# Up projection in runs of sixteen products of one width, and three buffers moved

## Chip, cores and metric

The kernel runs on one core of a Trainium2 chip. The metric is the device time of one execution in microseconds. A core has a matrix engine (TensorE, PE in the profile; its weight loads are PEld), a vector engine (DVE), a scalar engine (ACT), GpSimd (POOL) and a queue engine (SP) that here only issues DMAs. Each engine works through its own list of instructions in order and waits on semaphores for the others.

## The reference

Two layers. Each has a mixer (attention and a short convolution, with their projections) and then the part that this change touches, a squared-ReLU MLP. The sequence is 256 tokens, the model width 2048, the hidden width 8192, all in float32:

```python
for l in range(DEPTH):                      # DEPTH = 2
    h = _rmsnorm(x, attn_norm_g[l])
    ...                                     # attention and short convolution of h @ w_in[l]
    x = x + jnp.concatenate([attn, conv.astype(attn.dtype)], axis=-1) @ w_out[l]

    hm = _rmsnorm(x, mlp_norm_g[l]) @ w_up[l]          # (256, 2048) @ (2048, 8192)
    x = x + jnp.square(jax.nn.relu(hm)) @ w_down[l]    # (256, 8192) @ (8192, 2048)
```

## The kernel before

**Precision by parts.** A float32 operand is split into a high part `hi` (a rounded copy, made on ACT) and a low part `lo` (the rest, a subtraction on DVE that needs `hi`). A product of two such operands is made of three matmuls: high by high, high by low, low by high. For the up projection this is folded: the activations' high and low parts stand side by side, so one matmul with 512 columns multiplies the weights' high part with both (the wide product), and one with 256 columns multiplies the weights' low part with the activations' high part (the narrow product). Both go into the same PSUM bank, `upc`.

**The up stage** (`mlp`, from L999). It runs over 32 pairs `i` of hidden blocks. A pair has two columns `c` of 128 hidden units. A column sums over 16 blocks of 128 input features, in two halves `kh` of eight. `up_part(acc, kh)` (L942) takes one weight tile pair (`uhi`, `ulo`, made by `column`, L807, from a raw tile `uraw`) and issues eight wide and then eight narrow products (L952). So a column is eight wide, eight narrow, eight wide, eight narrow. `evict` (L960) copies the bank to `ev` on ACT (L962), which frees it, and adds its halves into `h` on DVE (L963). There is one such bank, so `ev` must be done before the next column starts. The first pair (`i == 0`) has its four half columns in another order, each with a call of its own.

After both columns `square` (L965) works on `h`, the tile of unrounded units: ReLU, a scale, a square, four sums `S1` to `S4`, for some pairs (`SEVEN`) a store of `h` to memory on POOL's queue (L982), and the rounding into `f` (L984 on ACT, L985 on DVE). `h` has one buffer.

**The quarters.** Two pairs later (`LAG = 2`), the units `f` are multiplied with two 128-row blocks of `w_down` over the first 1024 of its 2048 columns, by a scheme of seven products instead of eight (`product`, L992; matmuls at L995, tiles `pr`): products 1, 2, 3, 5 behind the pair's first column and 7, 6, 4 behind its second, each of three matmuls. Their weights come from `quarters` (L834) in three steps: `plain` loads the raw tile `draw` (L829, two DMAs of 512 KB on SP) and makes the plain parts `b1` and `b2`; `sums` makes the sums `t` and from them `t13`; `more` makes `t24`. Parts are made at L842 (ACT) and L843 (DVE). The raw tile is free after the last sum (L860). Before the change there are two raw tiles, two buffers of `b1` and `b2` each, and one of `t`, `t13` and `t24` each.

**The down stage** (from L1083) does what is left of the down projection: ordinary products (L1077, L1152) and, for the pairs in `SEVEN`, quarters over the other 1024 columns, with `h` loaded back into a tile `back` of the same pool and tag as `h`.

**What sets the order.** `weights.take()` (L357) hands out weight tiles in a fixed order of jobs and also lets the jobs up to three ahead be written (`AHEAD = 3`). High and low tiles have three buffers each. PE's instructions stand in the order of the program (`manual_schedule`). Those of the other engines, DMA issues included, are put in order when the kernel is built, by a scheduler that simulates the timeline; `late` (and `keep`) pins single instructions in program order. `work.tick()` lets pieces of background work go on; beside the up stage there is little of it.

Of the kernel before, what the change touches and what calls it, by code (L numbers as in the profile page):

```python
# [9 lines left out]
F32 = mybir.dt.float32  # L10
# [5 lines left out]
P = 128  # L16
# [12 lines left out]
CH = 512  # L29
WC = 256  # L30
KG = 4
# [74 lines left out]
def trunk(ctx: ExitStack, tc: tile.TileContext, x, w_in, w_out, conv_w, q_norm_g, k_norm_g,  # L106
          lambda_q1, lambda_k1, lambda_q2, lambda_k2, subln_g, attn_norm_g, mlp_norm_g,
          w_up, w_down, rel_bias, selector, out):
    nc = tc.nc
# [16 lines left out]
    def bank(name):  # L126
        return ps.tile([P, CH], F32, tag="bank", name=name)
# [4 lines left out]
    work = Background()  # L132
# [657 lines left out]
    def mlp(l, mnorm, last):  # L790
# [4 lines left out]
        mT = mnorm.tiles  # L795
        with ExitStack() as scope:
            upool = scope.enter_context(tc.tile_pool(name="upool", bufs=4))
            fpool = scope.enter_context(tc.tile_pool(name="fpool", bufs=2))
            dpool = scope.enter_context(tc.tile_pool(name="dpool", bufs=2))
            spool = scope.enter_context(tc.tile_pool(name="spool", bufs=1))  # L800
            work.start(mnorm.factors(), 1)

# [1 line left out]
            weights = Weights(upool)  # L804
            raws, forms = {}, {}
# [20 lines left out]
            def load_rows(i, col, pool=dpool, tag="draw"):  # L826
                raw = pool.tile([P, 2, 2 * CH], F32, tag=tag, name=tag)
                for k in range(2):
                    nc.sync.dma_start(  # L829
                        raw[:, k], w_down[l][(i * 2 + k) * P:(i * 2 + k + 1) * P,  # L830
                                             col:col + 2 * CH])
                return raw

            def quarters(i, col=0):  # L834


                keep = late if i == 0 or (i == SEVEN[0] and col) else lambda ins: None

                def parts(src, tag, bufs):
                    hi = spool.tile(list(src.shape), F32R, tag=f"{tag}h", name=f"{tag}h", bufs=bufs)  # L840
                    lo = spool.tile(list(src.shape), F32R, tag=f"{tag}l", name=f"{tag}l", bufs=bufs)
                    keep(nc.scalar.activation(hi, src, AF.Copy))  # L842
                    keep(nc.vector.tensor_sub(lo, src, hi.bitcast(F32)))  # L843
                    return hi, lo

                def plain():
                    raw = forms["raw"] = load_rows(i, col).rearrange("p k (n c) -> p k n c", n=2)
                    h1, l1 = parts(raw[:, 0, 0], "b1", 2)
                    h2, l2 = parts(raw[:, 1], "b2", 2)
                    return (h1, l1), (h2[:, 0], l2[:, 0]), (h2[:, 1], l2[:, 1])  # L850

                def sums():
                    raw = forms["raw"]
                    t = forms["t"] = spool.tile([P, 4, CH], F32, tag="t", name="t")

                    keep(nc.vector.tensor_sub(t[:, 0:2], raw[:, :, 1], raw[:, 0]))  # L856
                    h, lw = parts(t[:, 0:2], "t13", 1)

                    keep(nc.vector.tensor_add(t[:, 2], t[:, 1], raw[:, 0, 0]))
                    keep(nc.vector.tensor_sub(t[:, 3], raw[:, 1, 0], t[:, 2]))  # L860
                    return (h[:, 0], lw[:, 0]), (h[:, 1], lw[:, 1])

                def more():
                    h, lw = parts(forms["t"][:, 2:4], "t24", 1)
                    return (h[:, 0], lw[:, 0]), (h[:, 1], lw[:, 1])

                if (i, col) == (0, 0):
                    made = {}
                    forms["plain"] = lambda: made.update(p=plain())
                    forms["sums"] = lambda: made.update(s=sums())  # L870
                    return lambda: made["p"], lambda: made["s"], more
                return plain, sums, more

            def rows(i, k, box, col=0, *where):
# [63 lines left out]
            def column_bank():  # L938
                acc = ps.tile([P, CH], F32, tag="av", name="upc", bufs=1)
                return acc.rearrange("p (h s) -> p h s", h=2)  # L940

            def up_part(acc, kh):  # L942

                hi, lo = weights.take()
                for part, wt in ((0, hi), (1, lo)):
                    for k in range(8):
                        a = mT[kh * 2 + k // KG]
                        while not a.ready:  # L950
                            work.tick()
                        nc.tensor.matmul(  # L952
                            acc[:, 0] if part else acc, wt[:, k],
                            a.ap[:, 0, k % KG] if part else a.ap[:, :, k % KG],
                            start=(part == 0 and kh == 0 and k == 0),
                            stop=(part == 1 and kh == 1 and k == 7), skip_group_check=True)
                        if k % 4 == 3:
                            work.tick()

            def evict(acc, dst):  # L960
                ev = nat.tile([P, 2, S], F32, tag="wide", name="ev")
                nc.scalar.activation(ev, acc, AF.Copy)  # L962
                nc.vector.tensor_add(dst.rearrange("p a c -> p (a c)"), ev[:, 0], ev[:, 1])  # L963
# [35 lines left out]
            for i in range(NP):  # L999
                j = i - LAG  # L1000
                end = i == NP - 1
                h = fpool.tile([P, 8, P], F32, tag="h", name="h", bufs=1)
                if i == 0:
                    two = mm.tile([P, 2, CH], F32, tag="mm2", name="up0")
                    two = [two[:, c].rearrange("p (h s) -> p h s", h=2) for c in range(2)]
                    for kh in range(2):
                        for c in range(2):
                            up_part(two[c], kh)
                    forms["plain"]()
                    for c in range(2):  # L1010
                        evict(two[c], h[:, 2 * c:2 * c + 2])
                    fs[0] = square(0, h)
                    forms["sums"]()
                    continue
                for c in range(2):
                    if i < LAG:
                        acc = bank("upw").rearrange("p (h s) -> p h s", h=2)
                    else:
                        acc = column_bank()
                    up_part(acc, 0)  # L1020
                    up_part(acc, 1)
                    evict(acc, h[:, 2 * c:2 * c + 2])
                    if c == 1:
                        fs[i] = square(i, h)
                    if j == 0 and c == 0:
                        for pair in ((1, 6), (2, 3)):
                            w2 = mm.tile([P, 2, CH], F32, tag="mm2", name=f"pr{l}{pair[0]}")
                            prods[pair[0]], prods[pair[1]] = w2[:, 0], w2[:, 1]
                        for n in (5, 7, 4):
                            prods[n] = bank(f"pr{l}{n}")  # L1030
                    if j >= 0 and c == 0:
                        b11, b21, b22 = weights.take()
                        t1, t3 = weights.take()
                        f = fs[j]
                        product(1, f, A11, b11, j == 0, end)
                        product(2, f, A12, b21, j == 0, False)
                        product(3, f, S4, b22, j == 0, False)
                        product(5, f, S1, t1, j == 0, end)
                        work.tick()
                    elif j >= 0:  # L1040
                        t2, t4 = weights.take()
                        f = fs[j]
                        product(7, f, S3, t3, j == 0, end)
                        product(6, f, S2, t2, j == 0, end)
                        product(4, f, A22, t4, j == 0, False)
                        work.tick()
# [45 lines left out]
            def pair(i, f=None, at=0):  # L1092

                if f is None:
                    f = apool.tile([P, 2, 8, P], F32R, tag="a", name="fb")
                if i not in SEVEN:
                    nc.gpsimd.dma_start(
                        f[:, :, at:at + 4].rearrange("p a k c -> p a (k c)"), hid[i])
                    return f
                back = fpool.tile([P, 8, P], F32, tag="h", name="back", bufs=1)  # L1100
                nc.gpsimd.dma_start(back.rearrange("p a c -> p (a c)"), hid7[i])
                nc.scalar.activation(f[:, 0], back, AF.Copy)
                nc.vector.tensor_sub(f[:, 1], back, f[:, 0].bitcast(F32))
                return f
# [56 lines left out]
            for i in range(2 * BLK):  # L1161
# [7 lines left out]
                start, end = i == SEVEN[0], i == SEVEN[-1]  # L1169
# [89 lines left out]
```

## Time and profile before

| | us |
|---|---|
| median of 3 runs | 2139.8 (2139.35 to 2141.16) |
| the profiled execution, its own time | 2141.08 |
| its span, first to last instruction | 2139.3 |
| PE busy | 2130.0 |
| DVE busy | 1700.6 |
| ACT busy | 1317.1 |
| mean granted clock of TensorE | 1.000 |

In the profile the up stage of the first layer lies from about 391 to 895 us, that of the second from about 1454 to 1957. Busy time of PE is modelled: matmuls overlap, so a busy PE may still have products that stand further apart than need be. A row of the order of time gives start, length, engine, line, operation, `out<-in`, shape and count; in square brackets stands the idle time of the engine just before it and what ended it. A row of the stretches gives, for each engine, busy time and count, then the granted clock, the share of the DMA engines and GB/s.

### The profile page before, as it was taken

The page shows a single profiled execution, that of the slowest core. Times are in us where ns is not written, and L with a number is a line of the kernel's source. Part 1 is how long each engine was busy: PE and PEld are TensorE (multiplying, and loading weights), DVE is VectorE, ACT ScalarE, POOL GpSimd, SP SyncE. Part 2 cuts the span into 40 slices and gives each one's busy share as a digit, 9 for nine tenths or more (in the row PEclk, how much of TensorE's full clock was granted, in tenths as well). Part 3 has the DMA queues.
Part 4 walks back from the last instruction along what each step waited for, and adds up shares of the span by engine and source line. Part 5 has one row for each costly group of instructions (what it writes and reads, how often), then busy time and mean ns, then how long its engine had stood idle before and what let it go on. Part 6 is the DMA issues. An engine that isn't in the chain of part 4 may idle for free.

```text
span 2139.3 us, 29295 instructions
## 1 busy us (share of the span) xinstructions
PE 2130.0 (100%) x10925; PEld 1817.7 (85%) x10925; DVE 1700.6 (79%) x2316; ACT 1317.1 (62%) x1776; POOL 164.4 (8%) x226
## 2 busy tenths in 40 slices
PE   9999999999999999999999999999999999999999
PEld 8888888888888888888888888888888888888887
DVE  6778655798888888798766786557988888888986
ACT  6666445666666666565565765456666666665653
POOL 3110200000000000011111101000000000000110
PEclk9999999999999999999999999999999999999999
DMA  8555766577777777789656558656877777777983
GB/s 271 178 164 168 253 188 186 187 247 228 230 236 227 233 233 226 239 302 307 226 168 178 165 161 264 187 177 200 250 231 223 241 231 223 240 226 251 315 309 128
DMA packets 298254, 476.01 MB, mean 223 GB/s; under 512 B 12707, under 2 KB 193781, under 8 KB 298112
## 3 DMA queue, kind: packets, MB, share of 16 engines
q1 hardware_dynamic: 269120, 406.76, 60.8%
q0 software_dynamic: 28800, 67.24, 9.3%
q8 instruction: 85, 1.39, 0.3%
q14 instruction: 57, 0.47, 0.1%
q10 hardware_dynamic: 192, 0.15, 0.0%
HBM read 440.52 MB, written 33.58 MB: 222 GB/s over the span
## 4 chain that ended last, share of the span: by engine, by line
PE 97%; DVE 1%; ACT 1%; DMA 1%; issue 0%; DVEq 0%; ACTq 0%
PE upc L952 31%; PE pr L995 13%; PE dn L1077 8%; PE o L386 8%; PE gb L408 4%; PE k L386 4%; PE q L386 4%; PE v L386 4%; PE ci L408 4%; PE gc L408 4%; PE dn L995 2%; PE dn L1152 2%; PE pr1r L995 1%; PE pr0r L995 1%; PE upw L952 1%; PE up L952 1%
## 5 line engine op out<-in xcount | busy, mean ns | idle before, releaser
L303 DVE TENSOR_TENSOR wlo<-raw,whi 128x1024 fp32r<-128x1024 f32 x274 | 341.6, 1248 | 222.6 <-ACT whi L302 221.2
L302 ACT ACTIVATE whi<-raw 128x1024 fp32r<-128x1024 f32 x274 | 290.4, 1060 | 306.5 <-PE o L386 73.6
L952 PE MATMUL upc<-nT,uhi 128*128 128x512 f32 x1920 | 477.8, 391 | 1.1 <-ACT ev L962 1.1
L818 ACT ACTIVATE uhi<-uraw 128x1024 fp32r<-128x1024 f32 x256 | 271.3, 1061 | 283.3 <-PE upc L952 262.5
L952 PEld LDWEIGHTS upc<-nT,uhi 128*128 128x128 f32 x1920 | 352.6, 188 | 70.0 <-ACT ev L962 1.9
L819 DVE TENSOR_TENSOR ulo<-uraw,uhi 128x1024 fp32r<-128x1024 f32 x256 | 312.6, 1222 | 111.1 <-ACT uhi L818 107.3
L952 PEld LDWEIGHTS upc<-nT,ulo 128*128 128x128 f32 x1920 | 261.9, 190 | 18.7
L952 PE MATMUL upc<-nT,ulo 128*128 128x256 f32 x1920 | 267.7, 282 | 0.0
L1077 PE MATMUL dn<-whi,fb 128*128 128x512 f32 x528 | 166.1, 389 | 0.0
L386 PE MATMUL o<-whi,cat 128*128 128x512 f32 x512 | 159.5, 390 | 0.0
L302 ACT ACTIVATE whi<-uraw 128x1024 fp32r<-128x1024 f32 x66 | 70.1, 1062 | 87.4 <-PE dn L1077 79.3
L1077 PEld LDWEIGHTS dn<-whi,fb 128*128 128x128 f32 x528 | 99.1, 188 | 20.5
L386 PEld LDWEIGHTS o<-whi,cat 128*128 128x128 f32 x512 | 96.2, 188 | 19.7
L842 ACT ACTIVATE b2h<-draw 128x1024 fp32r<-128x1024 f32 x81 | 85.7, 1059 | 29.8 <-PE pr L995 22.0
L843 DVE TENSOR_TENSOR t13l<-t,t13h 128x1024 fp32r<-128x1024 f32 x81 | 99.2, 1224 | 6.1 <-ACT t13h L842 3.7
L1077 PE MATMUL dn<-wlo,fb 128*128 128x512 f32 x264 | 102.7, 389 | 0.0
L843 DVE TENSOR_TENSOR b2l<-draw,b2h 128x1024 fp32r<-128x1024 f32 x81 | 98.6, 1218 | 3.2 <-ACT b2h L842 3.2
L843 DVE TENSOR_TENSOR t24l<-t,t24h 128x1024 fp32r<-128x1024 f32 x81 | 98.8, 1219 | 1.5 <-ACT t24h L842 0.3
L386 PE MATMUL o<-wlo,cat 128*128 128x512 f32 x256 | 99.6, 389 | 0.0
L856 DVE TENSOR_TENSOR t<-draw 128x1024 f32<-128x1024 f32 x81 | 98.7, 1219 | 0.5
L303 DVE TENSOR_TENSOR wlo<-uraw,whi 128x1024 fp32r<-128x1024 f32 x66 | 80.5, 1222 | 21.7 <-ACT whi L302 15.3
L995 PE MATMUL pr<-t13h,f 128*128 128x512 f32 x240 | 93.8, 391 | 0.0
(408 smaller groups left out, 4111.3 us busy)
## 6 DMA issues: line engine op xcount, KB each, us to landing
uraw<-in_w_up_dram SPq DMA_DIRECT2D x128, 1024.0 KB, 6.5
raw<-in_w_in_dram SPq DMA_DIRECT2D x191, 512.0 KB, 3.9
draw<-in_w_down_dram SPq DMA_DIRECT2D x170, 512.0 KB, 4.6
uraw<-in_w_down_dram SPq DMA_DIRECT2D x66, 512.0 KB, 5.1
raw<-in_w_out_dram SPq DMA_DIRECT2D x64, 512.0 KB, 3.6
hid0p<-f POOLq DMA_DIRECT2D x20, 512.0 KB, 6.6
raw<-in_w_down_dram SPq DMA_DIRECT2D x10, 1024.0 KB, 5.1
fb<-hid0p POOLq DMA_DIRECT2D x20, 512.0 KB, 6.7
```

The lines of the kernel that those rows point to most:

```text
L302: pair = (nc.scalar.activation(hi, raw, AF.Copy), nc.vector.tensor_sub(lo, raw, hi.bitcast(F32)))
L303: nc.vector.tensor_sub(lo, raw, hi.bitcast(F32)))
L386: nc.tensor.matmul(acc[:, t], a.ap[:, pa, k % KG, t * P:(t + 1) * P], (hi, lo)[pw][:, j], start=(k == 0 and n == 0), stop=(k == nk - 1 and ...
L408: nc.tensor.matmul(acc[:, f, 0] if part else acc[:, f], wt[:, k % 4, fs], a.ap[:, 0, k % KG] if part else a.ap[:, :, k % KG], start=(part ...
L818: pair = (nc.scalar.activation(hi, src, AF.Copy), nc.vector.tensor_sub(lo, src, hi.bitcast(F32)))
L819: nc.vector.tensor_sub(lo, src, hi.bitcast(F32)))
L842: keep(nc.scalar.activation(hi, src, AF.Copy))
L843: keep(nc.vector.tensor_sub(lo, src, hi.bitcast(F32)))
L856: keep(nc.vector.tensor_sub(t[:, 0:2], raw[:, :, 1], raw[:, 0]))
L952: nc.tensor.matmul(acc[:, 0] if part else acc, wt[:, k], a.ap[:, 0, k % KG] if part else a.ap[:, :, k % KG], start=(part == 0 and kh == 0 ...
L995: nc.tensor.matmul(prods[n], f[:, pa, a], b[pw], start=(start and m == 0), stop=(stop and m == 2))
L1077: nc.tensor.matmul(prods[p], f[:, pa, 2 * k + t], b[pw][:, n], start=(p in starts and k == 0 and m == 0), stop=(stop and k == 1 and m == 2))
```

## The change

`up_part` takes both halves of a column at once, all wide products first and then all narrow ones: sixteen wide, sixteen narrow. The first pair still calls it with one half. The plain parts `b1` and `b2` get one buffer instead of two, the raw tile `draw` three instead of two, and `h` (with `back`) two instead of one. By their sizes per partition this is 12 KB less and 8 + 4 KB more. A quarter keeps its own `raw` and `t` in a dictionary `mine`.

```diff
-            dpool = scope.enter_context(tc.tile_pool(name="dpool", bufs=2))
+            dpool = scope.enter_context(tc.tile_pool(name="dpool", bufs=3))
...
+                mine = {}
...
-                    raw = forms["raw"] = load_rows(i, col).rearrange("p k (n c) -> p k n c", n=2)
-                    h1, l1 = parts(raw[:, 0, 0], "b1", 2)
-                    h2, l2 = parts(raw[:, 1], "b2", 2)
+                    raw = mine["raw"] = load_rows(i, col).rearrange("p k (n c) -> p k n c", n=2)
+                    h1, l1 = parts(raw[:, 0, 0], "b1", 1)
+                    h2, l2 = parts(raw[:, 1], "b2", 1)
...
-            def up_part(acc, kh):
-                hi, lo = weights.take()
-                for part, wt in ((0, hi), (1, lo)):
-                    for k in range(8):
-                        a = mT[kh * 2 + k // KG]
-                        while not a.ready:
-                            work.tick()
-                        nc.tensor.matmul(
-                            acc[:, 0] if part else acc, wt[:, k],
-                            a.ap[:, 0, k % KG] if part else a.ap[:, :, k % KG],
-                            start=(part == 0 and kh == 0 and k == 0),
-                            stop=(part == 1 and kh == 1 and k == 7), skip_group_check=True)
-                        if k % 4 == 3:
-                            work.tick()
+            def up_part(acc, *halves):
+                tiles = [weights.take() for _ in halves]
+                for part in range(2):
+                    for kh, wt in zip(halves, tiles):
+                        for k in range(8):
+                            a = mT[kh * 2 + k // KG]
+                            while not a.ready:
+                                work.tick()
+                            nc.tensor.matmul(
+                                acc[:, 0] if part else acc, wt[part][:, k],
+                                a.ap[:, 0, k % KG] if part else a.ap[:, :, k % KG],
+                                start=(part == 0 and kh == 0 and k == 0),
+                                stop=(part == 1 and kh == 1 and k == 7), skip_group_check=True)
+                            if k % 4 == 3:
+                                work.tick()
...
-                h = fpool.tile([P, 8, P], F32, tag="h", name="h", bufs=1)
+                h = fpool.tile([P, 8, P], F32, tag="h", name="h", bufs=2)
...
-                    up_part(acc, 0)
-                    up_part(acc, 1)
+                    up_part(acc, 0, 1)
...
-                back = fpool.tile([P, 8, P], F32, tag="h", name="back", bufs=1)
+                back = fpool.tile([P, 8, P], F32, tag="h", name="back", bufs=2)
```

More of the change, by code (lines that the diff above doesn't have):

```diff
@@ L846, in plain @@
                 def plain():
-                    raw = forms["raw"] = load_rows(i, col).rearrange("p k (n c) -> p k n c", n=2)
-                    h1, l1 = parts(raw[:, 0, 0], "b1", 2)
-                    h2, l2 = parts(raw[:, 1], "b2", 2)
+                    raw = mine["raw"] = load_rows(i, col).rearrange("p k (n c) -> p k n c", n=2)
+                    h1, l1 = parts(raw[:, 0, 0], "b1", 1)
+                    h2, l2 = parts(raw[:, 1], "b2", 1)
                     return (h1, l1), (h2[:, 0], l2[:, 0]), (h2[:, 1], l2[:, 1])
                 def sums():
-                    raw = forms["raw"]
-                    t = forms["t"] = spool.tile([P, 4, CH], F32, tag="t", name="t")
+                    raw = mine["raw"]
+                    t = mine["t"] = spool.tile([P, 4, CH], F32, tag="t", name="t")
                     keep(nc.vector.tensor_sub(t[:, 0:2], raw[:, :, 1], raw[:, 0]))
@@ L863, in more @@
                 def more():
-                    h, lw = parts(forms["t"][:, 2:4], "t24", 1)
+                    h, lw = parts(mine["t"][:, 2:4], "t24", 1)
                     return (h[:, 0], lw[:, 0]), (h[:, 1], lw[:, 1])
```

## Prediction

> **What bounds the kernel now.** I read the page first, then the list of who waited for whom, then the chain of waits, then the order of time on TensorE in single iterations.
>
> ```profile
> span 2139.3 us, 29295 instructions
> PE 2130.0 (100%) x10925; PEld 1817.7 (85%) x10925; DVE 1700.6 (79%) x2316; ACT 1317.1 (62%) x1776; POOL 164.4 (8%) x226
> PE 97%; DVE 1%; ACT 1%; DMA 1%; issue 0%; DVEq 0%; ACTq 0%
> L952 PE MATMUL upc<-nT,uhi 128*128 128x512 f32 x1920 | 477.8, 391 | 1.1 <-ACT ev L962 1.1
> ...
> PE upc L952 <- ACT ev L962: 1.1, 1, 1.1
> PE pr L995 <- DVE f L985: 0.9, 2, 0.5
> ```
>
> TensorE (PE) is 97% of the chain that ended last, and its waits in the up projection come to 2 us over both layers. So only two things can move the time: how fast PE gets through products that it could start at once, and those few stalls. Faster helpers buy nothing else; slower helpers cost only once a buffer runs dry. The last lines are from the list of waits on PE.
>
> **The new order of products.** One iteration of the up stage in order of time (columns: start, length of the group, engine, line, tiles, count):
>
> ```profile
> 719.98 1.98 PE L952 MATMUL upc<-nT,uhi 128*128 128x512 f32 x8
> 721.80 1.12 PE L952 MATMUL upc<-nT,ulo 128*128 128x256 f32 x8
> 722.75 2.00 PE L952 MATMUL upc<-nT,uhi 128*128 128x512 f32 x8
> 724.59 1.11 PE L952 MATMUL upc<-nT,ulo 128*128 128x256 f32 x8
> 725.54 0.40 PE L995 MATMUL pr<-b1h,f 128*128 128x512 f32 x1
> ...
> 721.80 0.28 PE L952 MATMUL upc<-nT,ulo 128*128 128x256 f32 x1
> 721.91 0.52 PE L952 MATMUL upc<-nT,ulo 128*128 128x256 f32 x3
> ```
>
> Lengths of groups overlap (matmuls are pipelined), so the time that a run takes is from its start to the next run's start. The wide run behind products of the same width takes 721.80 - 719.98 = 1.82 us; the one behind a narrow run takes 724.59 - 722.75 = 1.84. The narrow runs take 0.95 each. The chain of waits shows the same with less rounding:
>
> ```profile
> 404.05 11.17 PE upw L952 x64
> 440.92 5.56 PE upc L952 x32
> ...
> L952 PE MATMUL upw<-nT,uhi 128*128 128x512 f32 x64 | 16.0, 392 | 0.0
> ```
>
> A column whose first wide run also follows a narrow one takes 11.17 / 2 = 5.585 us; one that follows products takes 5.56. So going from narrow back to wide costs about 0.025 us. The change takes one such step out of each merged column. Against that, a narrow run of sixteen has no fresh start in its middle: inside a run the narrow products stand (0.52 - 0.28) / 2 = 0.12 us apart and the first two 0.11, so a start is worth up to 0.01, which is lost. After: 2 x 1.81 + 0.95 + 8 x 0.12 = 5.53 to 5.54 us against 5.56, that is 0.02 less, between 0.01 and 0.03. Merged columns: (1920 + 64) / 16 = 124, the groups "up" of each layer's first iteration being called with one half as before. **Term 1: 124 x 0.02 = -2.5 us** (-1.2 to -3.7).
>
> [...]
>
> **A third raw tile.** The largest stall is here (PE, then ACT, then the chain, then layer 1):
>
> ```profile
> 430.80 0.39 PE L995 MATMUL pr<-t24h,f 128*128 128x512 f32 x1
> 432.31 0.73 PE L952 MATMUL upc<-nT,uhi 128*128 128x512 f32 x2 [1.13 <-ACT ev L962]
> ...
> 430.20 0.63 ACT L842 ACTIVATE b1h<-draw 128x512 fp32r<-128x512 f32 x1 [2.69 <-DMA draw<-in_w_down_dram]
> 431.68 0.58 ACT L962 ACTIVATE ev<-upc 128x512 f32<-128x512 f32 x1
> ...
> 424.54 5.63 DMA draw<-in_w_down_dram
> ...
> 1494.14 0.39 PE L995 MATMUL pr<-t24h,f 128*128 128x512 f32 x1
> 1494.48 0.73 PE L952 MATMUL upc<-nT,uhi 128*128 128x512 f32 x2
> 1492.36 0.63 ACT L842 ACTIVATE b1h<-draw 128x512 fp32r<-128x512 f32 x1 [1.51 <-DMA draw<-in_w_down_dram]
> ```
>
> PE waits for the eviction `ev`, since the column's bank is single; `ev` stands on ACT behind `b1h`, which waits for a raw tile whose load could start only at 424.54, when the first of two raw tiles came free. With three, that load leaves near the stage's start. The stall is (432.31 - 430.80) - 0.23 = 1.28 us, plus 0.11 at the next product (0.73 - 0.39 = 0.34 apart instead of 0.23); in layer 1 it is (1494.48 - 1494.14) - 0.23 = 0.11, plus 0.11. **Term 2: -1.6 us** (0 to -1.6). What is late next there: `ev` could start when the column ends, ACT having been idle for 2.69 us, so nothing. The extra load is 1 MB on SP's queue ahead of the next `uraw` loads; its price is bounded by the 5.63 us of the draw load above, and I take none.
>
> **A second buffer for unrounded units.** The tile `h` is held from a unit's sum until its rounding `f` and, for some units, its store. Twice `f` is late for its products:
>
> ```profile
> 470.11 0.40 PE L995 MATMUL pr<-b1l,f 128*128 128x512 f32 x1
> 470.97 0.50 PE L995 MATMUL pr<-b1h,f 128*128 128x512 f32 x1 [0.47 <-DVE f L985]
> 471.31 0.40 PE L995 MATMUL pr<-b2h,f 128*128 128x512 f32 x1
> 1533.15 0.50 PE L995 MATMUL pr<-b1h,f 128*128 128x512 f32 x1 [0.47 <-DVE f L985]
> ...
> 453.77 0.76 DVE L963 TENSOR_TENSOR h<-ev 128x256 f32<-128x256 f32 x2
> ...
> 432.31:448.25 15.94, 15.94 (x85) 13.79 (x86) 15.43 (x21) 11.68 (x15) 0.55 (x1) 1.00 0.72 220
> ```
>
> The second column of that unit ended at 440.92 + 5.56 = 446.48, but both sums into `h` ran at 453.77, behind the unit before. A second `h` lets them go earlier; 0.75 us earlier is enough. Each stall is 0.86 - 0.23 = 0.63 plus 0.11, the same 0.47 bracket standing in both layers. **Term 3: 2 x 0.74 = -1.5 us** (0 to -1.5); I take all of it, less surely than term 2, since DVE is nearly full there: the last row is a stretch of one iteration, with 15.43 us of DVE in 15.94.
>
> **One buffer for the plain parts.** Now `b1` and `b2` are made two iterations ahead, right after the products that free them; then one ahead, at the same moments. In the up stage:
>
> ```profile
> 726.76 0.62 ACT L842 ACTIVATE b1h<-draw 128x512 fp32r<-128x512 f32 x1
> 727.81 1.06 ACT L842 ACTIVATE b2h<-draw 128x1024 fp32r<-128x1024 f32 x1 [0.43 <-PE pr L995]
> 729.53 1.22 DVE L843 TENSOR_TENSOR b2l<-draw,b2h 128x1024 fp32r<-128x1024 f32 x1
> ...
> 932.74 1.23 DVE L843 TENSOR_TENSOR b2l<-draw,b2h 128x1024 fp32r<-128x1024 f32 x1 [0.26 <-ACT b2h L842]
> 938.45 0.39 PE L995 MATMUL pr0r<-b1h,fb 128*128 128x512 f32 x1
> ```
>
> The refill ends at 730.75; the next products of this kind come one iteration (15.94 us) after 725.54, at 741.5. Cover: 10.7 us. In the down stage, where quarters are closest, the refill ends at 933.97 and the next use is 938.45: 4.5 us. Cost nothing; without that cover each such quarter would lose at most the 1.22 us of the `b2l` row. The two refills that now run before the first products become one, which relieves DVE there.
>
> **Taking two weight tiles at once.** The high tile of the second half is needed 1.8 us into the column instead of 2.8; the one made at 722.00 (row below) is used in the column after this one, over 8 us later. That row also gives the lag from a release on PE to the start on ACT, 722.00 - 721.80 = 0.2. The low tile of the first half is freed at 3.62 + 0.95 = 4.57 us instead of 2.77, and the low conversion that refills it waits that much longer; behind it on DVE stand sums of `t`, of `h` and the rounding of `f`, for which PE waits two products later at the earliest. DVE in this iteration:
>
> ```profile
> 719.14:735.08 15.94, 15.94 (x87) 13.78 (x86) 14.11 (x20) 10.69 (x15) 0.00 (x0) 1.00 0.68 215
> ...
> 722.00 1.06 ACT L818 ACTIVATE uhi<-uraw 128x1024 fp32r<-128x1024 f32 x1 [0.45 <-PE upc L952]
> 723.58 1.22 DVE L819 TENSOR_TENSOR ulo<-uraw,uhi 128x1024 fp32r<-128x1024 f32 x1
> 731.39 1.23 DVE L819 TENSOR_TENSOR ulo<-uraw,uhi 128x1024 fp32r<-128x1024 f32 x1 [0.44 <-ACT uhi L818]
> 734.19 1.23 DVE L819 TENSOR_TENSOR ulo<-uraw,uhi 128x1024 fp32r<-128x1024 f32 x1 [1.36 <-ACT uhi L818]
> ```
>
> The first row gives DVE 14.11 us busy of 15.94. Suppose its order stayed as it is. The conversion of 723.58 could start at 719.98 + 4.57 + 0.2 = 724.75. The next column starts twelve products of 0.23 after 725.54, at 728.29, so the one of 731.39 could start at 728.29 + 4.77 = 733.06. Between those two lie 8.31 us and 731.39 - 723.58 - 0.44 = 7.37 of work; from the second to the next iteration's first, 7.63 us and (739.52 - 731.39) - 1.36 = 6.77 of work. Both fit, with 0.9 to spare, so PE sees nothing. Cost zero; the bounds are 0 and rival 1.
>
> **Sum.** -2.5 - 1.6 - 1.5 = -5.6 us. The profiled execution took 2141.08 us with a span of 2139.3; it lies 1.3 over the median 2139.8, so I take the difference off the median: 2134.2 (from the profiled one, 2135.5). The runs before lie within 1.8 us; about 0.2%, 4.3 us, is what a measurement of this kernel can tell from no change. Beyond it lie 2135.5 and 2144.1.
>
> **Rivals.** 1, slower: the low tile freed 1.8 us later blocks DVE, because the new order puts a low conversion in front of more work than the 0.9 us of room allows. It comes in 58 iterations with products (29 a layer). It decides from -5.6 + 58 x > 4.3, x = 0.17 us over the room per iteration; at 0.2 it gives 2139.8 - 5.6 + 11.6 = 2145.8. For it: DVE is 88% busy and its order is the scheduler's, not mine. Against it: the replay above. 0.19.
>
> 2, partial: terms 1 and 2 come, but `f` or an eviction is still late at the ramp, DVE being full there: 2139.8 - 4.1 = 2135.7, and with a new stall of 1 to 3 us 2136.7 to 2138.7. 0.23.
>
> 3, the order is free (the step from narrow to wide moves elsewhere in the column): 2139.8 - 3.1 = 2136.7. Against it stands the 5.585 to 5.56 of the chain. [...] 0.08.
>
> My forecast, all three terms: 0.50.
>
> **Numbers.** Forecast 2134.2. Its own range: terms 2 and 3 whole, term 1 between its bounds: 2133.0 to 2135.5. The 8-in-10 range takes in rivals 2 and 3 and the near end of rival 1: 2132.8 to 2141.0. Faster by over 0.2%: the forecast, 0.50. Within: rivals 2 and 3, 0.31. Slower: rival 1, 0.19.
>
> **What would show it.** Term 1: two groups x16 per column, wide then narrow, and 5.54 us from a column's start to its products. Term 2: no ACT idle ended by a draw load near 430 and 1492, and no PE idle ended by `ev`. Term 3: the row "pr L995 <- DVE f" gone. DVE's longest waits would move to `ulo <- PE upc`. I am wrong if an iteration in the middle takes 15.94 us or more, or if new rows of PE waits stand at L952 or L995.

## The result and the profile after

| | before | after |
|---|---|---|
| median, us | 2140.48 (2138.78 to 2141.87) | 2151.38 (2150.56 to 2152.8) |
| runs, on the same chip | 6 | 6 |
| span of the profiled execution, us | 2139.3 | 2149.4 |
| mean granted clock of TensorE | 1.000 | 0.997 |

The changed kernel is slower: ratio 1.0055 [1.0044, 1.0066], 10.9 us. The forecast was 5.6 us faster, and the time lies beyond the range. The page after:

```profile
span 2149.4 us, 29197 instructions
PE 2130.2 (99%) x10925; PEld 1820.8 (85%) x10925; DVE 1696.2 (79%) x2316; ACT 1350.2 (63%) x1776; POOL 164.7 (8%) x226
```

The span is 10.1 us longer and TensorE is as busy as before, to 0.2 us, so the page alone would have one look for time in which it stands. The list of waits on TensorE has it. The rows that were to go are gone (`ev` at the up projection, `f` at L995), and two new ones stand first (in total, times, longest, us):

```profile
PE pr L1079 <- ACT f L987: 6.6, 2, 3.3
PE pr L1079 <- DVE f L988: 6.5, 2, 3.2
```

L1079 is the line of the down stage's ordinary products (L1077 before). Two waits, once a layer each: one place. So I measured each stretch of TensorE from its first product to the next stretch's first:

| stretch, us | first layer before | after | second layer before | after |
|---|---|---|---|---|
| pair `i = 1` of the up stage (`upw`) | 11.17 | 11.13 | 11.17 | 11.13 |
| rest of the up stage, from `i = 2` | 480.19 | 476.83 | 479.03 | 476.83 |
| the first 48 ordinary products | 10.88 | 19.98 | 10.88 | 20.03 |
| rest of the down stage | 170.32 | 169.96 | 171.00 | 170.62 |

The pair `i = 0` takes 12.25 us in both kernels. The up stage became 5.6 us shorter over both layers, the sum forecast. The 48 products behind it became 18.3 us longer. (The rest is -0.7 in the down stage and -1.8 in the mixers, where a wait of TensorE for a weight part, 1.0 us in the execution before, varies from one execution to another: 0 after, 1.5 in a run below.)

The order of time on TensorE in the middle of the up stage, and a row of one column from the chain of waits:

```profile
723.82 3.79 PE L955 MATMUL upc<-nT,uhi 128*128 128x512 f32 x16
727.45 2.08 PE L955 MATMUL upc<-nT,ulo 128*128 128x256 f32 x16
729.36 0.40 PE L998 MATMUL pr<-t13h,f 128*128 128x512 f32 x1
```

```profile
422.01 5.54 PE upc L955 x32
```

A column takes 729.36 - 723.82 = 5.54 us instead of 5.56, an iteration 15.90 instead of 15.94. Now the stage's end, on TensorE, ACT and DVE:

```profile
890.36 0.39 PE L1079 MATMUL pr<-whi,f 128*128 128x512 f32 x1
...
895.57 0.39 PE L1079 MATMUL pr<-whi,f 128*128 128x512 f32 x1
899.24 0.50 PE L1079 MATMUL pr<-whi,f 128*128 128x512 f32 x1 [3.28 <-ACT f L987]
899.58 0.40 PE L1079 MATMUL pr<-wlo,f 128*128 128x512 f32 x1
903.20 1.22 PE L1079 MATMUL pr<-whi,f 128*128 128x512 f32 x2 [3.23 <-DVE f L988]
...
907.85 0.39 PE L1079 MATMUL pr<-wlo,f 128*128 128x512 f32 x1
...
888.01 1.07 ACT L1104 ACTIVATE fb<-back 128x1024 fp32r<-128x1024 f32 x1 [0.37 <-PE upc L955]
...
898.56 0.63 ACT L987 ACTIVATE f<-h 128x512 fp32r<-128x512 f32 x1
...
889.87 1.22 DVE L1105 TENSOR_TENSOR fb<-back,fb 128x1024 fp32r<-128x1024 f32 x1
891.00 1.22 DVE L858 TENSOR_TENSOR t<-draw 128x1024 f32<-128x1024 f32 x1
892.14 0.42 DVE L966 TENSOR_TENSOR h<-ev 128x256 f32<-128x256 f32 x1
...
895.71 1.22 DVE L845 TENSOR_TENSOR t13l<-t,t13h 128x1024 fp32r<-128x1024 f32 x1
896.84 0.69 DVE L861 TENSOR_TENSOR t<-t,draw 128x512 f32<-128x512 f32 x1
897.44 0.42 DVE L974 TENSOR_TENSOR h<-h,ratiob 128x256 f32<-128x256 f32 x1
...
902.46 0.69 DVE L988 TENSOR_TENSOR f<-h,f 128x512 fp32r<-128x512 f32 x1
```

TensorE stands for (899.24 - 895.57) - 0.23 = 3.44 us until the last unit's `f` has its high part, and for (903.20 - 899.58) - 0.23 = 3.39 until it has its low part. Ahead of the scale of `h` (897.44) and of that low part stands work for the down stage's first quarter on DVE: `fb` from `back`, the first sum `t`, `t13l` and a second sum, and behind them, ahead of the low part alone, low weight parts and a third sum. The same place before:

```profile
899.67 0.68 DVE L985 TENSOR_TENSOR f<-h,f 128x512 fp32r<-128x512 f32 x1
...
907.83 1.21 DVE L1103 TENSOR_TENSOR fb<-back,fb 128x1024 fp32r<-128x1024 f32 x1
908.96 1.21 DVE L856 TENSOR_TENSOR t<-draw 128x1024 f32<-128x1024 f32 x1
...
900.65 0.56 POOL L1101 DMA_DIRECT2D back<-hid0s  x1 [8.85 <-DVE f L985]
```

There `fb` and `t` come 8 us behind `f`, because the load of `back` on POOL's queue waited for that same `f`: `back` shares the tag of `h`, and the one buffer was free only when the last unit had been rounded. After:

```profile
882.58 0.56 POOL L1103 DMA_DIRECT2D back<-hid0s  x1 [7.54 <-DVE f L988]
```

Counted from the first ordinary product (895.25 before, 890.36 after), with two buffers the load leaves 13 us earlier, the release now being the `f` of the unit before the last, and its conversions stand on ACT and DVE in front of the last unit's work. The stretches of the stage's end (granted clock in the third column from the right) show the rest of the price:

```profile
890.36:899.30 8.94, 5.66 (x26) 4.38 (x24) 8.94 (x13) 5.06 (x7) 0.56 (x1) 1.00 0.88 301
903.20:907.70 4.50, 4.50 (x11) 3.55 (x12) 3.84 (x4) 0.43 (x1) 0.54 (x1) 0.51 0.52 168
```

DVE is busy for all 8.94 us, TensorE for 5.66. Behind the second stall TensorE runs at 0.51 of its clock: from 903.20 to 907.85 are eleven products, which take 2.50 us at 0.227 and took 4.65. So 3.44 + 3.39 + 0.11 (the product after the first stall) + 2.15 = 9.1 us a layer.

### The profile page after: what moved, and what is told of

Same layout as the page of the kernel before. It is cut to its first block, busy times and chain, and to the rows that moved or that the text cites. A ratio compares the mean times of both kernels' runs of the same rounds, so it can differ in the third digit from the quotient of the medians.

```text
span 2149.4 us, 29197 instructions
## 1 busy us (share of the span) xinstructions
PE 2130.2 (99%) x10925; PEld 1820.8 (85%) x10925; DVE 1696.2 (79%) x2316; ACT 1350.2 (63%) x1776; POOL 164.7 (8%) x226
## 4 chain that ended last, share of the span: by engine, by line
PE 97%; DVE 1%; ACT 1%; issue 1%; DVEq 0%; ACTq 0%
PE upc L955 31%; PE pr L998 13%; PE dn L1079 8%; PE o L386 8%; PE ci L408 4%; PE gb L408 4%; PE k L386 4%; PE q L386 4%; PE v L386 4%; PE gc L408 4%; PE dn L1154 2%; PE dn L998 2%; PE pr1r L998 1%; PE pr0r L998 1%; PE up L955 1%; PE upw L955 1%
## 5 line engine op out<-in xcount | busy, mean ns | idle before, releaser
L955 PE MATMUL upc<-nT,uhi 128*128 128x512 f32 x1920 | 454.7, 389 | 0.0
L955 PEld LDWEIGHTS upc<-nT,uhi 128*128 128x128 f32 x1920 | 360.3, 188 | 74.7
L955 PEld LDWEIGHTS upc<-nT,ulo 128*128 128x128 f32 x1920 | 246.2, 191 | 9.3
L955 PE MATMUL upc<-nT,ulo 128*128 128x256 f32 x1920 | 249.1, 283 | 0.0
L1079 PE MATMUL dn<-whi,fb 128*128 128x512 f32 x528 | 166.1, 389 | 0.0
L1079 PEld LDWEIGHTS dn<-whi,fb 128*128 128x128 f32 x528 | 99.1, 188 | 20.5
L965 ACT ACTIVATE ev<-upc 128x512 f32<-128x512 f32 x120 | 71.9, 599 | 51.9 <-PE upc L955 51.9
L844 ACT ACTIVATE t24h<-t 128x1024 fp32r<-128x1024 f32 x81 | 86.2, 1064 | 28.9 <-PE pr L998 15.9
L1079 PE MATMUL dn<-wlo,fb 128*128 128x512 f32 x264 | 102.7, 389 | 0.0
```

The costliest lines, as they stand in the source:

```text
L955: nc.tensor.matmul(acc[:, 0] if part else acc, wt[part][:, k], a.ap[:, 0, k % KG] if part else a.ap[:, :, k % KG], start=(part == 0 and kh ...
L1079: nc.tensor.matmul(prods[p], f[:, pa, 2 * k + t], b[pw][:, n], start=(p in starts and k == 0 and m == 0), stop=(stop and k == 1 and m == 2))
```

## The experiments

Three theories of the loss. **A**: the second `h`, by its tag, lets `back` go ahead of the last `f`. **B**: the new order frees low tiles later and so delays DVE (rival 1 of the prediction). **C**: the third raw tile lets the next quarter's sums go ahead.

**The order alone.** From the changed kernel (only the parts of the lines that differ):

```diff
-name="dpool", bufs=3      "b1", 1   "b2", 1      tag="h", name="h", bufs=2      name="back", bufs=2
+name="dpool", bufs=2      "b1", 2   "b2", 2      tag="h", name="h", bufs=1      name="back", bufs=1
```

> The new order of products alone: columns of sixteen wide and sixteen narrow products, with the buffers as before (two raw tiles, two of the plain parts, one of h). Theory A (the second h lets the tile back of the down stage load early, and its conversions then stand on DVE and ACT ahead of the rounding f of the last pair): no stall at the end of the up stage, 2.4 us less than before from the order (124 columns x 0.02), the stalls on the draw load and on f near 430 and 470 stay, so about 2138 against 2140.5. Theory B (the low tiles freed later by the new order push work on DVE back, and the last f with it): the 9 us per layer at the end of the up stage are here, about 2156.

Measured 2138.84 us (11 runs) against 2140.27 (27), ratio 0.9996 [0.9987, 1.0005]. The stage's end takes 10.88 us as before: B falls, the new order brings no loss. It brings less than the 2.5 us of term 1 too: the rest of the up stage takes 479.29 and 478.92 us, 0.9 and 0.1 less than before. TensorE waits longer in the ramp, as the up stage's first iterations are called here (its list of waits):

```profile
PE upc L955 <- ACT ev L965: 2.5, 2, 1.4
PE pr L998 <- DVE t13l L845: 0.8, 2, 0.4
```

The wait for `ev` was 1.1 us in all before, the one for `t13l` is new, and the one for `f`, which was expected to stay, is gone without a second `h`. So with a new order of products the other engines' work falls differently too, and small stalls come and go with it; TensorE isn't earlier at `ev` (40.2 us after the stage's first product, 39.5 before). Why the stalls fall as they do here was not tested.

**The buffers alone.**

```diff
-                    up_part(acc, 0, 1)
+                    up_part(acc, 0)
+                    up_part(acc, 1)
```

> The three buffers as changed, but columns of eight wide, eight narrow, eight wide, eight narrow as before. Theory A: the stalls at the end of the up stage are here (two of 3.4 us a layer and a stretch at half clock, 9.1 us a layer), the stalls near 430 and 470 are gone (-3.1): 2140.5 + 18.3 - 3.1 = about 2156. Theory B: no stall at the end, -3.1, about 2137.4.

Measured 2154.18 us, ratio 1.0063 [1.0051, 1.0076]. The list of waits on TensorE has the whole loss in the old order:

```profile
PE pr L1080 <- ACT f L987: 6.4, 2, 3.2
PE pr L1080 <- DVE f L988: 6.0, 2, 3.2
```

The end takes 20.59 and 19.53 us. The up stage, rid of stalls in both kernels, takes 478.03 in the old order and 476.83 in the new: term 1 by itself is 1.2 us a layer and 0.04 in the pair `i = 1`, 2.5 in all.

**One `h`.** (Parts of two lines.)

```diff
-tag="h", name="h", bufs=2      name="back", bufs=2
+tag="h", name="h", bufs=1      name="back", bufs=1
```

> The changed kernel with one buffer of h and back instead of two; third raw tile, single plain parts and new order stay. Theory A: no stall at the end of the up stage; order -2.4, draw load -1.6, the two stalls on f (1.5 together) stay: about 2136.5. Theory C (the third raw tile lets the sums of the first quarter of the down stage in early, ahead of the last f): the 9 us per layer stay, about 2153. Theory B: they stay too.

Measured 2142.12 us, ratio 1.0009 [1.0001, 1.0018]. The end takes 10.88 in both layers: the loss there goes with the second `h`, as A has it. The time was missed all the same, for a stall that I had put at 0.74 us grew (waits, then the order of time, on TensorE; then DVE; then the store of `h` in the list of DMA issues, with its size and the time from issue to landing, before and here):

```profile
PE pr L998 <- DVE f L988: 4.8, 2, 2.4
```

```profile
467.88 0.40 PE L998 MATMUL pr<-b1l,f 128*128 128x512 f32 x1
470.65 0.50 PE L998 MATMUL pr<-b1h,f 128*128 128x512 f32 x1 [2.38 <-DVE f L988]
...
457.82 0.76 DVE L966 TENSOR_TENSOR h<-ev 128x256 f32<-128x256 f32 x2 [1.34 <-DMA hid0s<-h]
```

```profile
hid0s<-h POOLq DMA_DIRECT2D x1, 512.0 KB, 3.7
```

```profile
hid0s<-h POOLq DMA_DIRECT2D x1, 512.0 KB, 10.9
```

With one `h` a pair's sums wait until the pair before is rounded and, here, stored. The store takes 10.9 us to land instead of 3.7. A load of `uraw` and the two of a raw tile `draw` leave 1.3, 0.7 and 0.3 us ahead of it here, and all three left behind it before; whether they are what slows it was not tested. Counted from the stage's first product, the low part of `f` so ends 0.8 us later than before (80.0 against 79.3), and TensorE, without the stall on `ev`, arrives 1.1 us earlier (77.6 against 78.7). It waits 2.54 us, and then, from some 1.2 us after it has begun again, runs at half clock (0.50 from 472.10 to 475.30). The up stage behind its pair `i = 1` is 481.55 us long; the second `h` takes 4.7 a layer from it.

**Two raw tiles.**

```diff
-dpool = scope.enter_context(tc.tile_pool(name="dpool", bufs=3))
+dpool = scope.enter_context(tc.tile_pool(name="dpool", bufs=2))
```

> The changed kernel with two raw tiles instead of three; two buffers of h, single plain parts and the new order stay. Theory A (the second h, through back, is what brings the work in early): the stalls at the end of the up stage are here in the main part. As built, DVE does the conversion of back ahead of the last sum into h, and two more conversions and a sum t stand ahead of the low part of f, which puts that part some 3 us late: one stall of about 3.4 us a layer, perhaps with a stretch at half clock (2.4 us) behind it. With -2.4 for the order and the draw stalls staying: 2140.5 - 2.4 + 7 to 12 = 2145 to 2150. Theory C (the third raw tile brings it in): no stall at the end, about 2138.

Measured 2147.65 us against 2140.46 (10 runs), ratio 1.0035 [1.0021, 1.0049]. The end takes 17.27 and 17.16 us, so 6.3 to 6.4 of the 9.1 us are there without the third tile. On DVE:

```profile
889.49 1.22 DVE L1105 TENSOR_TENSOR fb<-back,fb 128x1024 fp32r<-128x1024 f32 x1
...
896.33 1.23 DVE L858 TENSOR_TENSOR t<-draw 128x1024 f32<-128x1024 f32 x1
...
898.68 0.69 DVE L988 TENSOR_TENSOR f<-h,f 128x512 fp32r<-128x512 f32 x1
```

`fb` still comes ahead of `f`, but the sum `t` starts 5.7 us later, counted from the first ordinary product (889.98 here): its load was issued at 888.5, when a raw tile came free, and landed at 896.2. C is a lesser part of A: the third tile adds 2.8 us a layer to a loss that needs the second `h`. The up stage takes 476.83 us, as with three tiles.

**The early work held back.** All of the change, and the first conversions of `back` put behind the last `f` on ACT and DVE. `behind` lets what stands in it be issued only after the instructions in `last_f`; its definition is left out here:

```diff
-                nc.scalar.activation(f[:, 0, :n], h[:, :n], AF.Copy)
-                nc.vector.tensor_sub(f[:, 1, :n], h[:, :n], f[:, 0, :n].bitcast(F32))
+                last_f[:] = [nc.scalar.activation(f[:, 0, :n], h[:, :n], AF.Copy),
+                             nc.vector.tensor_sub(f[:, 1, :n], h[:, :n], f[:, 0, :n].bitcast(F32))]
...
-                nc.scalar.activation(f[:, 0], back, AF.Copy)
-                nc.vector.tensor_sub(f[:, 1], back, f[:, 0].bitcast(F32))
+                with behind(i == SEVEN[0]):
+                    nc.scalar.activation(f[:, 0], back, AF.Copy)
+                    nc.vector.tensor_sub(f[:, 1], back, f[:, 0].bitcast(F32))
```

> The changed kernel with one thing added: the two conversions of the first tile back of the down stage (one on ACT, one on DVE) are queued behind the rounding f of the last pair on their engines. All buffers and the order of products as changed. Theory A: the stalls at the end of the up stage go, all three gains stay: 2140.5 - 5.6 = about 2134.9. Theory B and theory C: the 9 us per layer stay, about 2151.

Measured 2136.43 us, ratio 0.9982 [0.9973, 0.9991]: 15 us less than the changed kernel, with the same buffers and the same order of products. The end takes 10.88 us again. In order of time on DVE, the last row on TensorE:

```profile
895.31 0.68 DVE L989 TENSOR_TENSOR f<-h,f 128x512 fp32r<-128x512 f32 x1
...
898.25 1.22 DVE L1114 TENSOR_TENSOR fb<-back,fb 128x1024 fp32r<-128x1024 f32 x1
...
905.43 1.21 DVE L846 TENSOR_TENSOR t13l<-t,t13h 128x1024 fp32r<-128x1024 f32 x1
907.17 2.35 DVE L303 TENSOR_TENSOR wlo<-raw,whi 128x1024 fp32r<-128x1024 f32 x2
...
908.43 0.50 PE L1163 MATMUL dn<-wlo,f 128*128 128x512 f32 x1 [0.81 <-DVE wlo L303]
```

That A is the cause is shown: the edit moves only `fb`'s two conversions, the load of `back` leaves as early as in the changed kernel, and the sum `t`, which is kept in program order, stands behind `fb` again (899.39). The time is 1.5 us above the forecast, for a small stall of the same kind is left (last row): `t13l` and a sum stand ahead of a low weight part that TensorE needs sooner.

**These held back too.** Besides the above, that quarter's `t13` parts and its later sums are put behind the first four weight pairs of the down stage (`raw4`, collected in lines left out here):

```diff
+                    with behind(i == SEVEN[0] and col, raw4):
+                        h, lw = parts(t[:, 0:2], "t13", 1)
...
+                        keep(nc.vector.tensor_add(t[:, 2], t[:, 1], raw[:, 0, 0]))
+                        keep(nc.vector.tensor_sub(t[:, 3], raw[:, 1, 0], t[:, 2]))
```

> The changed kernel with the conversions of the first back queued behind the last f, and besides that the later sums and the t13 parts of the first quarter of the down stage queued behind the first four low weight parts of that stage. Against the version with the first of the two alone, which has a stall of 0.97 + 0.11 us a layer at the start of the down stage, where PE waits for a low weight part that stands on DVE behind t13l and a sum: that stall should go, about 2 us for both layers, so some 2134.4. If DVE is short of time there whatever the order, another wait comes in its place near the first quarter and the time stays at 2136.4.

Measured 2133.86 us, ratio 0.9970 [0.9959, 0.9982]: faster than both kernels, 6.6 us under the one before. The stage's end as a stretch (PE busy 22.00 of 22.00, clock 1.00), and all that TensorE still waits for, which is outside the part changed:

```profile
890.00:912.00 22.00, 22.00 (x99) 18.20 (x98) 21.68 (x28) 12.05 (x14) 2.13 (x4) 1.00 0.89 293
```

```profile
PE ci L410 <- ACT whi L302: 1.5, 2, 1.0
PE sc L606 <- DVE cat L684: 1.2, 2, 0.6
PE warm L160 <- DVE mhalf L152: 1.1, 1, 1.1
```

**One buffer of plain parts alone.** The runs so far left open which part took away the stall on `ev`: the third raw tile, as my prediction had it, or (theory **D**) the single buffer of plain parts. From the new order with the buffers as before:

```diff
-h1, l1 = parts(raw[:, 0, 0], "b1", 2)      h2, l2 = parts(raw[:, 1], "b2", 2)
+h1, l1 = parts(raw[:, 0, 0], "b1", 1)      h2, l2 = parts(raw[:, 1], "b2", 1)
```

> New order, two raw tiles and one h as before, and only the buffers of the plain parts b1 and b2 changed, from two to one. In the runs so far the wait of TensorE for the eviction ev in the ramp (1.28 us before, 1.4 us twice with the new order alone) is absent wherever the plain parts have one buffer, with two raw tiles as with three, and the draw loads of the changed kernel leave when they left with two raw tiles. Theory D, the single plain buffer takes the stall away, since the conversion b1h of the next quarter can no longer stand on ACT ahead of ev: no row of TensorE waiting for ev at L955; the up stage behind its first columns is 481.5 us long in each layer, as in the run with one h, because the longer stall on f in the ramp (2.4 us) comes with the single plain buffer; down stage starts without a stall (10.88); total about 2142. Rival, as my prediction had it, the third raw tile takes it away: two stalls of about 1.4 us on ev stay, as with the new order alone, and the up stage is about 478.9; total about 2139.

Measured 2142.83 us against 2139.93 (16 runs), ratio 1.0011 [1.0002, 1.0021]. On TensorE no wait for `ev` is left, with two raw tiles, and the up stage behind its pair `i = 1` is 481.56 and 481.58 us long, as D had it. That is 2.3 and 2.7 us more than with the order alone: the store of `h` takes 11.1 us here, against 3.2 there, and the stall on `f` is the longer one. ACT in this kernel:

```profile
428.39 0.60 ACT L965 ACTIVATE ev<-upc 128x512 f32<-128x512 f32 x1 [0.85 <-PE upc L955]
```

`ev` now waits for its column alone. Before, `b1h` of the next quarter stood ahead of it, waiting for a load; with one buffer `b1h` has no place to write to so early.

**The faster version with two raw tiles.**

```diff
-dpool = scope.enter_context(tc.tile_pool(name="dpool", bufs=3))
+dpool = scope.enter_context(tc.tile_pool(name="dpool", bufs=2))
```

> The faster version (all parts of the change, with the down stage's early work held back behind the last f and the first raw weight parts), but with two raw tiles draw as before. Theory D, the third raw tile does nothing for the up stage: 476.83 us in each layer as with three, the stretch at the stage's end 10.88 and the total 2133.9 within 1 us. Rival, the third raw tile carries term 2 of the prediction: a stall of 1.3 to 1.6 us returns in the up stage, total 2135.5 or more.

Measured 2133.45 us, ratio 0.9970 [0.9959, 0.9981], with 476.83 and 10.88 us in both layers: beside single plain parts the third raw tile brings nothing.

**Not tried.** `back` with a buffer and a tag of its own; the second `h`, or the third raw tile, together with two buffers of plain parts.

## Why the prediction was wrong

**The step that failed** is "A second buffer for unrounded units". It asked what the buffer would end (the stalls on `f`), and not what it would let begin. That `h` and `back` share pool and tag stood in the description of the kernel, but no term of the sum had a price for `back`'s load, its two conversions and the pinned sums behind them. Their price is 9.1 us a layer, 18.3 in all, against 5.6 gained. What was late next was asked of ACT at the draw stall, but not at the end of the stage, where before the last `f` had 0.8 us to spare: it ended 900.35 - 895.25 = 5.1 us after the first ordinary product, and TensorE needs its low part about 5.9 after it (5.44 for the high part, then two products).

**Term 1** was right: 2.5 us forecast, 2.5 measured with the other stalls out of the way, by sixteen wide, sixteen narrow, and 5.54 us a column. Rival 3 falls: the order isn't free. The single starts show where the step lies: in the kernel before, at 722.75, the first five of the wide products behind narrow ones stand 233, 236, 228, 233 and 231 ns apart and the later ones 227, and the first two gaps of a narrow run are 113 and 119 ns instead of 120. Gathering widths saves the first and gives up the second.

**Term 2** had the right stall, and its load did what was forecast, but the stall didn't hang on it. A quarter's raw tile takes two DMAs. With three raw tiles SP's queue sends three quarters' loads at the stage's start, and with two tiles two quarters' there and the third later. The changed kernel, and then the one with two raw tiles:

```profile
390.70 4.53 SPq L829 DMA_DIRECT2D draw<-in_w_down_dram  x6
```

```profile
390.33 3.47 SPq L829 DMA_DIRECT2D draw<-in_w_down_dram  x4
...
422.33 0.82 SPq L829 DMA_DIRECT2D draw<-in_w_down_dram  x2
```

So the third quarter's load leaves some 28 us sooner with the third tile; that the draw loads leave when they left with two raw tiles, as the expectation for the single plain buffer has it, holds only from the load behind it on. Yet the stall on `ev` goes with two raw tiles as well, by "One buffer for the plain parts", which I had put at nothing. Whether the third raw tile beside two plain buffers would have ended it too, no run shows.

**Term 3** was right in kind and its size depends on the rest. Taken alone from the kernel before, the two stalls are 1.5 us. With the stall on `ev` gone TensorE arrives earlier, the store that frees the one `h` lands later, and the second `h` is worth 4.7 us a layer. In steps, from the up stage's lengths: order alone -0.9 and -0.1, single plain buffer +2.3 and +2.7, second `h` -4.7 and -4.8, third raw tile 0. That the sum came out as forecast is partly luck: the stalls of this chain didn't add up part by part.

**"Taking two weight tiles at once" at nothing** was right, and rival 1, the one on the slower side, was slower by another mechanism than the true one: iterations take 15.90 us with the later low tiles, and the order alone brings no loss. Its price, 2145.8, would have been too low as well. Neither sign of being wrong that the prediction named has come: iterations got shorter, and no new wait stands at the up projection or its products. One sign of being right failed to come: `ulo <- PE upc` isn't among DVE's longest waits. The prediction looked for a loss inside the up stage only; the loss is at L1079, among the first ordinary products behind it.

## What to carry to other kernels

Before adding a buffer, list every tile of its pool and tag, and ask for each which load the extra buffer sets free, and what that load's consumers will then stand in front of on the in-order queues. Look above all at the stage's last unit, where the next stage's first work can go ahead of it; if the buffer is worth having, hold that work back with an order edge (a rule that one instruction is queued behind another) instead of giving the buffer up. When several small stalls lie in one chain, test them together: with one gone, the next can be longer (here the wait on the low part of `f` went from 0.47 to 2.38 us).

## What the runs showed of the hardware

**Stalls that cost clock behind them.** With one `h`, in the stretches before, at and behind the stall of 2.4 us idle, the granted clock is:

```profile
467.90:470.65 2.75, 0.37 (x2) 0.00 (x0) 2.72 (x4) 0.08 (x1) 0.00 (x0) 1.00 0.54 137
470.65:472.10 1.45, 1.45 (x6) 1.20 (x7) 0.99 (x3) 0.91 (x2) 0.67 (x1) 0.92 1.01 341
472.10:475.30 3.20, 3.20 (x9) 2.48 (x8) 2.47 (x7) 2.43 (x4) 0.16 (x1) 0.50 0.67 222
```

A mean of 0.92 over 1.45 us is half clock for the last 0.2 of them, so the clock fell to half, as an estimate from these rows, some 1.2 us after work had begun again. It stayed there for 3.4 us (the 0.2 and the 3.20 of the last row, at 0.50), half of which, 1.7 us, is lost. Behind the 1.1 us idle at 432.31 before it stayed at 1.00 (stretch from 432.30 to 436.00). Behind the 1.4 us idle at 431.97 with the order alone nine wide products took 2.37 us, where at half clock products stand 0.43 us apart (472.80 and 473.23 with one `h`); the mean clock of that execution is 1.000, against 0.998 with one `h`. Of the stalls in these runs those of 1.1 and 1.4 us idle left the clock as it was, and those of 2.4 us (here) and 3.4 us (two raw tiles, 0.50 from 899.40 to 905.20) had half clock behind them. Where between 1.4 and 2.4 us that begins, and whether it depends on more than the idle time, isn't shown.

**In-order queues.** DVE and ACT took up their work here in the order in which it was queued. In the changed kernel the low part of `f`, whose high part was ready at 899.19 (898.56 + 0.63), started on DVE at 902.46, 3.27 us later, behind low weight parts and a sum queued ahead of it. In the kernel before, ACT stood idle for 2.69 us up to `b1h` at 430.20, which waited for a load, and took up `ev` behind it at 431.68, though `ev`'s column had ended by 429.12.
